# Attention scores of two heads in the two halves of the array's rows, in a two-layer diffusion backbone on one core

## The chip, the cores and the metric

The kernel runs on one core of a Trainium2 chip. Its engines are TensorE (PE, with its weight loads shown apart as PEld), VectorE (DVE), ScalarE (ACT), GpSimd (POOL) and SyncE (SP), which issues most of the transfers from HBM. The metric is the time of one execution on the device, in microseconds.

## The reference

Two layers work on 256 latent tokens and 256 context tokens of 1024 features. A layer is a pair of token mixers (windowed attention with a sink, and a bidirectional gated linear recurrence), gated, projected and normed, and then a mixture of 16 experts, of which each takes 32 tokens of a stream. What matters here is the attention: 8 heads of 64 features, with two groups of keys and values, so that four heads share one set of keys.

```python
HEAD_DIM = 64; ATTN_HEADS = 8; ATTN_KV_HEADS = 2; WINDOW = 128
...
    s_win = jnp.einsum('bntgrd,bnsgd->bngrts', qb, kw) * scale
    s_win = jnp.where(valid[None, :, None, None], s_win, -jnp.inf)
    s_ctx = jnp.einsum('bntgrd,bcgd->bngrtc', qb, kc) * scale
    m = jnp.maximum(jnp.maximum(s_ctx.max(-1), s_win.max(-1)), s_sink)
    ...
    o = (einsum(e_ctx, vc) + einsum(e_win, vw)) / denom
```

A latent token sees its window and the whole context, 512 keys with the mask. A context token (first layer only; the second needs no context output) sees the 256 context keys.

## The kernel before

The function `front(l, ...)` is the mixer of a layer, `moe(l, ...)` its experts. Features lie on the partitions in the mixer: `qT[:, i, :]` holds the queries of heads 2 i and 2 i + 1, the even one on partitions 0 to 63, the odd one on 64 to 127. `kT` holds the keys of a group twice, `kT[:, 2 g]` with the keys on partitions 0 to 63 and zeros below, `kT[:, 2 g + 1]` the other way round. A product of all 128 rows of `qT[:, i]` with one of the two then is the score of one head, the other head meeting zeros. The zeros are written by two memsets in `kv_in`, the keys by four copies in `blk_ka`, two by VectorE and two by ScalarE.

`attention(s, i2, ...)` works on 128 queries of a stream. For each group `g` it takes four heads: the score product into a bank of PSUM (`scb()`, the tag `sc`, two banks), for latent queries the mask (L693), the maximum (L696), the exponential (L701), a scaling (L705), the transposes through another bank (L708) and their copy (L709). After the four heads the products with the values go to a tile `po`, which is also a bank `sc` (L713), and are copied out (L716). The first layer has four such calls, two with 512 keys and two with 256; the second has two with 512. That makes 48 score products.

Most other matmuls in the mixers are `mm3` (L163 to L165): float32 accuracy by three products of split operands. The score products, the transposes and the expert products are plain float32. Several lines divide the array by columns: L713 writes two halves of 64 output partitions, L283 (the modulation, whose steps fill idle times of PE), L527 and L594 write quarters of 32.

The order of the work on each engine's queue is set when the program is built, by a planner that plays the program on a timeline and takes, for an engine that is free, the first ready instruction in the order of the program; `hg_chain` is moved ahead with `tc.high_priority`. Within an engine's queue the order is then fixed. The expert weights are loaded by SyncE in one order (`in_order(loads, ...)`), each as soon as its place is free.

Of the kernel before, what the change touches and what calls it, by code (L numbers as in the profile page):

```python
# [89 lines left out]
def _view(t, offset, pattern):  # L90
    # a strided view of a tile: offset and pattern in elements of one partition
    return bass.AP(tensor=t.tensor, offset=t.offset + offset, ap=[list(t.ap[0])] + pattern)


class HL:
    # a float32 array as the sum of two float32r arrays
# [8 lines left out]
def tile_kernel(ctx, tc, x, c, ctx_in, c_ctx, w_mod, b_mod, w_in, attn_sink, lb_fw, lb_bw, norm_g,  # L105
# [47 lines left out]
    def in_order(chain, ins):  # L153
        # instructions of a chain stay in the order of the program in their engine's queue
        if chain:
            tc.add_manual_dep(ins.ins, chain[0].ins.name,
                              mybir.DependencyInfo(mybir.DependencyClass.NoSync, mybir.DependencyReason.DATA),
                              reason="order")
        chain[:] = [ins]

    def mm3(p, a, b, start, stop, **kw):
        # a^T b in float32 accuracy: the product of the low parts is below its last bit
        mm(p, a.hi, b.hi, start=start, stop=False, **kw)  # L163
        mm(p, a.hi, b.lo, start=False, stop=False, **kw)  # L164
        mm(p, a.lo, b.hi, start=False, stop=stop, **kw)  # L165

    # ---------------------------------------------------------------- constants, small vectors
    # the conditions first: what all else waits on
# [15 lines left out]
    # silu(c), silu(c_ctx) as stationary columns, padded to 32  # L184
# [19 lines left out]
    # lower bounds of the forget gates of the second layer (those of the first are 0): columns (dir, head)  # L204
# [16 lines left out]
    # ---------------------------------------------------------------- modulation, as columns  # L221
    # (section * 2 + half, 128-block, stream); sections 1 and 4 hold 1 + scale
# [11 lines left out]
    def mod_cols(l, pm, a, q0, dq, ns):  # L234
        # chunks q0, q0 + dq: quarters of 256 columns, each on the partitions 32 j + stream
        nc.vector.tensor_copy(a, pm[:, 0:256])
        pt = mdb()
        for m in range(2):
            nc.tensor.transpose(pt[:, 128 * m:128 * m + 128], a[:, 128 * m:128 * m + 128], ident)
        pv = pt[:, 0:256].rearrange("p (m q j r) -> p q j m r", m=2, q=2, j=2)  # L240
        for s in range(ns):
            for q in range(2):
                nc.vector.tensor_tensor(MT[l][:, q0 + dq * q, :, s].rearrange("p (j m) -> p j m", j=2), pv[:, q, :, :, s],
                                        BM[:, l, q0 + dq * q].rearrange("p (j m) -> p j m", j=2), op=ALU.add)

    def mod_first(M0, g):
        # the shifts and scales of a quarter of the features in layer 0
# [19 lines left out]
    def mod_steps(l, q0, ns):  # L267
        # chunks q0, q0 + 1 of the streams: a step for each 128 rows, whose products take PE's idle times
# [24 lines left out]
    def bcast_rows(l, sec, dst, S, after=()):  # L293
        # dst [128, S, 1024]: section 2 (g1) or 5 (g2), the same on every partition
# [10 lines left out]
    # ---------------------------------------------------------------- layer norm  # L305
# [39 lines left out]
    def ln_affine2(dst, src, lnp, mu, r, seq):  # L345
        # from a pair of banks
# [14 lines left out]
    def transposed(xh, s, k, sink_fn, p):  # L361
        # features [128 k, 128 k + 256) of the two token tiles of a stream, modulated by sink_fn
# [49 lines left out]
    # ---------------------------------------------------------------- token mixers  # L412
    def front(l, fillers, X=None, finish=None):
# [16 lines left out]
        # the last of the fillers wait for PE's idle times in the routing  # L430
# [6 lines left out]
        def filler(f):  # L437
            # the transfer of a step runs a step ahead of its products
            if f:
                f[0](WM)  # L440
                behind.append(f[1])
            if len(behind) > 0 or not f and behind:
                behind.pop(0)(WM)
# [29 lines left out]
        def cols_tile(*segs, busy=None):  # L473
            # columns of w_in, in one tile of 256
# [10 lines left out]
        def fm(w, j, n, p=None, ks=range(KT)):  # L485
            # features (128 columns j of the tile w) by n tokens
# [5 lines left out]
        # ---- HGRN: one head  # L492
        # axis of directions: 0 backward, 1 forward
# [18 lines left out]
        def hg_chain(h, q, K, F):  # L512
            # decayed scores, keys by queries: AT (within 128 tokens), A1 (tile to tile), A2 (context to x)
# [9 lines left out]
            def sums(Pr, sel, p, start, stop):  # L523
                # sums over features, to each of the 32 keys of a block that sel takes
# [12 lines left out]
            # level 0: a token with itself, both directions  # L537
# [10 lines left out]
            def update(m):  # L548
                # from blocks of m to blocks of 2 m: decay over the other half
# [18 lines left out]
            # levels 1 and 2: products of single pairs, summed over features  # L568
            for i, m in ((1, 1), (2, 2)):
                p = hsb()  # L570
                for j in range(m):
                    Pr = tp("Pr")[:, :TQ]
                    n = TQ // (2 * m)
                    # queries of a second half with key j of the first half (forward)
                    nc.vector.tensor_tensor(_view(Pr, m, [[2 * m, n], [1, m]]), _view(Q, TQ + m, [[2 * m, n], [1, m]]),
                                            _view(K, 512 + j, [[2 * m, n], [0, m]]), op=ALU.mult)
                    # queries of a first half with key j of the second half (backward)
# [5 lines left out]
            # levels 4, 8, 16: blocks of 32 keys by 32 queries; forward keys in first halves, backward in second  # L583
# [17 lines left out]
            # blocks of 32 and of 64 within a tile  # L601
# [23 lines left out]
            # tile to tile: 0 from the second tile to the first (backward), 1 from the first to the second  # L625
# [8 lines left out]
            # context to x, the sum of both directions  # L634
# [33 lines left out]
        # ---- attention  # L668
# [9 lines left out]
        def attention(s, i2, qT, kT, va):  # L678
# [5 lines left out]
            for g in range(2):  # L684
                eT = C.tile([128, 4, 4, 128], F32, name="eT")
                for i in range(4):
                    hd = 4 * g + i
                    par = i % 2
                    p = scb()
                    mm(p[:, :nk], qT[:, hd // 2, tk], kT[:, 2 * g + par, k0:k0 + nk], start=True, stop=True)  # L690
# [27 lines left out]
        # ---- the schedule of one front  # L718
        C, kT, va, ihv = None, None, None, None

        def chains():
            nonlocal C, kT, va, ihv
            C = pool(sC, f"C{l}")
            kT = C.tile([128, 4, 512], F32, name="kT")
# [8 lines left out]
        def blk_ka(w, j):  # L733
# [4 lines left out]
            for g in range(2):  # L738
                for h in range(2):
                    (nc.scalar.copy if h else nc.vector.tensor_copy)(kT[64 * h:64 * h + 64, 2 * g + h, :],  # L740
# [44 lines left out]
        def kv_in():  # L785
            nc.gpsimd.memset(kT[64:128, 0:4:2, :], 0.0)
            nc.gpsimd.memset(kT[0:64, 1:4:2, :], 0.0)
# [14 lines left out]
        def second(s):  # L802
            # the inputs of the second layer, a stream, in tiles that are free yet; of the context no more is needed
# [57 lines left out]
        else:  # L861
            with ExitStack() as s0:
                xh0 = xh_first(s0)
                M0 = pool(s0, "M0")
                for g in range(5):
# [7 lines left out]
                    # the first head's products as far as the features are there  # L873
                    for i in range(4 if g else 0):
                        fm(ws0[i // 2], i % 2, TQ, ps0[i], range(2 * g - 2, 2 * g))
                # the other constants
# [23 lines left out]
        # ---- branches, gates  # L900
# [59 lines left out]
        # ---- output projection, residual, post norm  # L960
# [11 lines left out]
        # the last token tiles take the first half of w_out first, which is not needed any more then  # L972
# [14 lines left out]
    # ---------------------------------------------------------------- mixture of experts  # L987
    def moe(l, X, M, slots):
# [5 lines left out]
        def eload(src, e):  # L994
            # an expert's matrix in four tiles of 256 rows
# [8 lines left out]
        def eload_cols(src, e):  # L1004
            # an expert's matrix in four tiles of 256 columns
# [15 lines left out]
        # the router's weights for the plain norm of a stream: scaled; the shift's share apart  # L1021
# [12 lines left out]
        def route(s):  # L1034
# [5 lines left out]
            for i in range(2):  # L1040
                t = 2 * s + i
                ln_plain(xh[:, t, :], X[t], i == 0)
                # logits, transposed, in four partial sums; then summed, tokens on partitions
# [27 lines left out]
            # the taken tokens in their order: 1, 2, ..., the others 0  # L1071
# [11 lines left out]
        def onehot(gi, s):  # L1083
            # the slots of the four experts of a group, as one-hot rows of the tokens
# [8 lines left out]
        def weights(gi, s):  # L1093
            # the weighted one-hot rows of a group, slots on partitions
# [7 lines left out]
            if gi == 3 and s == 0:  # L1102
                # the last expert's rows once more, for every share of its products
# [11 lines left out]
        def gather(gi, s, after=()):  # L1115
            # rows of the four experts of a group, feature-major, modulated
# [38 lines left out]
        def end_begin():  # L1155
            # the rows of the first stream with all but the last expert's share
# [9 lines left out]
        def end_products(c, py, hT, w, Yc):  # L1166
            # a quarter of the features of the last expert, the blocks of rows in shares
# [7 lines left out]
        def end_first(c, Yc):  # L1175
            # their share of the first stream
# [7 lines left out]
        def end_second(c, Yc):  # L1184
            # the rows of the second one in their place
# [4 lines left out]
        G = 2 if S == 2 else 4          # column groups of the array  # L1190
        MW = 128 // G                   # slots of an expert (both streams)
        NW = FF // G                    # width of a column group's share
        NB = NW // 128
        for gi in range(4):
            for e4 in range(4):
# [43 lines left out]
                if e == 0:  # L1239
                    late = M["late"]()  # L1240
                    Y, g2 = late["Y"], late["g2"]
                    # g2, its stream as the rows of the products of an expert have it
# [36 lines left out]
        def finish_out():  # L1279
            # the output in halves of the rows, one of them on other engines  # L1280
# [29 lines left out]
    def moe_pools(l, st, S, zones, right=()):  # L1310
        # zones: the pools from the bottom, each a list of names of tiles and of numbers of weight slots
# [4 lines left out]
        for z, names in enumerate((right,) + zones if right else zones):  # L1316
            Z = pool(sZ, f"ZR{l}", side="right") if names is right else pool(st, f"Z{l}{z}")
            for n in names:
                if isinstance(n, int):
                    for i in range(n):  # L1320
                        # the place of WM has 1 KB more than its one slot
                        w = 2304 if z == 2 + (right != ()) else 2048
                        slots.append(lambda Z=Z, i=i, w=w: Z.tile([128, w], F32, name=f"w{i}", tag=f"w{i}")[:, :2048])
                elif n not in shapes:
                    # what is not needed before the end of the first expert: a slot until then
                    once.append(lambda Z=Z, n=n: Z.tile([128, 2048], F32, name="w" + n, tag=n))
                    parts.append((n, lambda Z=Z, n=n: Z.tile([128, 2048], F32, name=n, tag=n)))
                else:
                    M[n] = Z.tile([128] + shapes[n], F32, name=n, tag=n)
                    if n == ("xh" if l else "xs"):  # L1330
                        # the place is free when they are loaded
# [19 lines left out]
    with ExitStack() as st:  # L1351
        M, s, once = moe_pools(0, st, 2, ([4], [2], [1], [3], ["g2 OH", 3], ["xh", 3]), ("Y", "xs", "oT"))
        # the slot in the place of the last modulation's weights comes later than the others
        a, b, c = s[7:10] + s[13:16], s[10:13], s[0:6]
        # in the order of release: the second expert's first products come before the first one's last
# [40 lines left out]
```

## Time and profile before

| | us |
|---|---|
| median of three runs | 1835.53 |
| lowest and highest run | 1832.83, 1835.88 |
| span of the profiled execution (first to last instruction) | 1832.6 |
| PE busy in it | 1579.6 |
| mean granted TensorE clock, as a share of full speed | 0.914 |

The profiled execution's own time outside its span is not recorded; the lowest run is 0.2 us above the span. Stages of that execution: mixer of the first layer to about 460 us, its experts to about 1000, mixer of the second layer to about 1345, its experts to the end.

### The profile page before, as it was taken

What the parts mean: (1) busy time and instruction counts of PE and PEld (TensorE: products, weight loads), DVE (VectorE), ACT (ScalarE), POOL (GpSimd) and SP (SyncE); (2) the same over time, 40 slices, a digit from 0 to 9 for tenths busy, and PEclk for the clock granted to TensorE, in tenths of its full rate; (3) what the DMA queues carried; (4) which work ended last, traced back from release to release, by engine and by line L of the source; (5) the groups of instructions that cost most, each with busy time, mean ns of one, the idle gap of its engine ahead of it and who ended that gap; (6) DMA issues with size and microseconds to landing.
All of it is one profiled execution on the core that took longest, in us unless ns stands there. A gap on an engine that the chain in (4) does not pass through costs nothing. (4 is left out here: it accounts for less than half of the span.)

```text
span 1832.6 us, 27361 instructions
## 1 busy us (share of the span) xinstructions
PE 1579.6 (86%) x11339; PEld 921.2 (50%) x11339; DVE 681.1 (37%) x1425; ACT 449.7 (25%) x850; POOL 304.9 (17%) x300
## 2 busy tenths in 40 slices
PE   6999999999989998997988999998968766766675
PEld 4777776688754433332223788775844322322222
DVE  5546566324651211211213756666651110101102
ACT  2436556323120100001001533576410000000000
POOL 2342121224300000000002633331610000000001
PEclk9999999999989999999999999999978866776777
DMA  9544124524679999999999653325689999999997
GB/s 320 183 117 125 60 81 133 202 91 150 258 300 399 409 409 409 409 409 409 409 409 371 213 174 112 122 81 175 239 341 410 409 409 409 409 408 409 409 409 283
DMA packets 207372, 526.06 MB, mean 287 GB/s; under 512 B 9736, under 2 KB 93904, under 8 KB 207248
## 3 DMA queue, kind: packets, MB, share of 16 engines
q1 hardware_dynamic: 205136, 517.46, 75.3%
q0 software_dynamic: 1392, 4.49, 0.7%
q10 hardware_dynamic: 720, 2.36, 0.4%
q8 instruction: 89, 1.46, 0.3%
q14 instruction: 35, 0.29, 0.0%
HBM read 523.23 MB, written 1.05 MB: 286 GB/s over the span
## 5 line engine op out<-in xcount | busy, mean ns | idle before, releaser
L1204 PE MATMUL acc<-w,xs 128*32 128x256 f32 (+1 forms) x3064 | 419.4, 530 | 102.0 <-DMA w<-in_w_up_dram 56.9
L1204 PEld LDWEIGHTS acc<-w,xs 128*32 128x32 f32 (+1 forms) x3064 | 139.1, 134 | 366.5 <-issue 178.1
L1237 PE MATMUL o<-w,hT 128*32 128x256 f32 (+1 forms) x1432 | 196.5, 534 | 43.0 <-DMA w<-in_w_down_dram 29.2
L163 PE MATMUL acc<-uTh,wh 128*128 128x512 f32 (+1 forms) x592 | 215.0, 365 | 2.4 <-ACT sgs L829 1.5
L164 PE MATMUL acc<-uTl,wh 128*128 128x512 f32 (+1 forms) x592 | 212.0, 358 | 0.5 <-DVE uTl L387 0.5
L165 PE MATMUL acc<-uTh,wl 128*128 128x512 f32 (+1 forms) x592 | 210.7, 356 | 0.0
L1215 ACT ACTIVATE h<-acc 128x512 f32<-128x512 f32 (+1 forms) x32 | 15.7, 490 | 534.2 <-PE acc L1204 521.4
L1237 PEld LDWEIGHTS o<-w,hT 128*32 128x32 f32 (+1 forms) x1432 | 65.8, 136 | 153.2 <-issue 74.0
L468 POOL TENSOR_TENSOR wl<-win,wh 128x1024 fp32r<-128x1024 f32 x44 | 113.7, 2584 | 164.0 <-ACT wh L467 162.4
L1216 DVE TENSOR_TENSOR h<-h,acc 128x512 f32<-128x512 f32 (+1 forms) x32 | 17.7, 552 | 308.7 <-PE acc L1204 308.7
L163 PEld LDWEIGHTS acc<-uTh,wh 128*128 128x128 f32 x592 | 111.8, 190 | 27.0 <-issue 7.1
L165 PEld LDWEIGHTS acc<-uTh,wl 128*128 128x128 f32 x592 | 112.3, 190 | 17.7 <-issue 3.4
L164 PEld LDWEIGHTS acc<-uTl,wh 128*128 128x128 f32 x592 | 112.3, 190 | 17.5 <-issue 3.1
L467 ACT CAST wh<-win 128x1024 fp32r<-128x1024 f32 x84 | 84.0, 1046 | 84.3 <-PE acc L164 61.7
L1096 POOL TENSOR_TENSOR OW<-OH,aff 128x256 f32<-128x256 f32 x8 | 4.9, 615 | 598.5 <-PE sc L1219 583.6
L1260 DVE TENSOR_TENSOR Y<-o,g2 OH 32x512 f32<-32x512 f32 x60 | 41.2, 687 | 141.0 <-PE o L1237 140.3
L468 DVE TENSOR_TENSOR wl<-win,wh 128x1024 fp32r<-128x1024 f32 x40 | 53.5, 1338 | 79.7 <-ACT wh L467 78.9
L1221 ACT COPY hT<-sc 128x512 f32<-128x512 f32 (+1 forms) x32 | 15.3, 479 | 256.1 <-PE sc L1219 256.1
L1260 DVE TENSOR_TENSOR Y g<-o,Y g 32x256 f32<-32x256 f32 x60 | 25.2, 420 | 128.0 <-PE o L1237 127.3
L283 PE MATMUL md<-wmod,scol 128*32 128x256 f32 x640 | 57.6, 414 | 6.6 <-DMA wmod<-in_w_mod_dram 5.2
L553 DVE TENSOR_TENSOR K<-K,F 128x512 f32<-128x512 f32 x56 | 46.6, 832 | 8.7 <-PE hs L619 5.3
L322 POOL TENSOR_TENSOR mv<-mv,nhalf 128x1 f32<-128x1 f32 x26 | 24.4, 943 | 130.6 <-DVE mv L321 125.4
(448 smaller groups left out, 2360.1 us busy)
## 6 DMA issues: line engine op xcount, KB each, us to landing
w<-in_w_gate_dram SPq DMA_DIRECT2D x128, 1024.0 KB, 18.6
w<-in_w_up_dram SPq DMA_DIRECT2D x127, 1024.0 KB, 18.5
w<-in_w_down_dram SPq DMA_DIRECT2D x127, 1024.0 KB, 18.6
wmod<-in_w_mod_dram SPq DMA_DIRECT2D x80, 512.0 KB, 4.6
win<-in_w_in_dram SPq DMA_DIRECT2D x26, 1024.0 KB, 6.3
win<-in_w_in_dram SPq DMA_DIRECT2D x32, 512.0 KB, 5.4
wmod<-in_w_mod_dram SPq DMA_DIRECT2D x32, 256.0 KB, 6.2
wo<-in_w_out_dram SPq DMA_DIRECT2D x8, 1024.0 KB, 5.8
```

What stands on the lines that cost most here:

```text
L163: mm(p, a.hi, b.hi, start=start, stop=False, **kw)
L164: mm(p, a.hi, b.lo, start=False, stop=False, **kw)
L165: mm(p, a.lo, b.hi, start=False, stop=stop, **kw)
L283: mm(pm[32 * j:32 * j + 32, 0:256], scol[:, k, :], w[:, 256 * j:256 * j + 256], start=(k == 0), stop=(k == KT - 1))
L322: pows.append(nc.gpsimd.tensor_tensor(mv[:, 2:3], mv[:, 2:3], nhalf[:, 0:1], op=ALU.pow))
L467: nc.scalar.copy(hi[:, r], w[:, r])
L468: ins = eng.tensor_sub(lo[:, r], w[:, r], hi[:, r])
L553: nc.vector.tensor_tensor(kv, kv, _view(f, 0, [[nf + 1, 2], [2, nf // 2], [0, m]]), op=ALU.mult)
L1204: ins = mm(p[MW * j:MW * j + MW, :NW], xs[:, k, e4, :], wrow(w, k)[:, NW * j:NW * j + NW], start=(k == 0), stop=(k == KT - 1))
L1216: nc.vector.tensor_mul(h, h, pu[:, :NW])
L1237: mm(py[MW * dj:MW * dj + MW, :NW], hT[:, 128 * m + MW * j:128 * m + MW * j + MW], wrow(wd, kt)[:, NW * dj:NW * dj + NW], start=(kt == 0), ...
L1260: nc.vector.tensor_tensor(o, py[r:r + 32, :NW], g2[r:r + 32, NW * dj:NW * dj + NW], op=ALU.mult)
```

## The change

The keys are stored once a group, `kT[0:64, g]` and `kT[64:128, g]` holding the same keys, and there are no zeros and no memsets. The scores of an even head and of the odd one after it are two products of 64 rows, one from partitions 0 to 63 of `qT` and `kT`, the other from 64 to 127, written one after the other in the program ahead of the work on either head, into two banks `sc`. The mask, the softmax, the transposes and the products with the values are as before, head by head. Comments, which the diff also takes out, are left out here.

```diff
@@ attention(s, i2, qT, kT, va)
                 for i in range(4):
                     hd = 4 * g + i
                     par = i % 2
-                    p = scb()
-                    mm(p[:, :nk], qT[:, hd // 2, tk], kT[:, 2 * g + par, k0:k0 + nk], start=True, stop=True)
+                    if par == 0:
+                        sc = [scb(), scb()]
+                        for h in range(2):
+                            r = slice(64 * h, 64 * h + 64)
+                            mm(sc[h][:, :nk], qT[r, hd // 2, tk], kT[r, g, k0:k0 + nk], start=True, stop=True)
+                    p = sc[par]
@@ chains()
-            kT = C.tile([128, 4, 512], F32, name="kT")
+            kT = C.tile([128, 2, 512], F32, name="kT")
@@ blk_ka(w, j)
-                    (nc.scalar.copy if h else nc.vector.tensor_copy)(kT[64 * h:64 * h + 64, 2 * g + h, :],
+                    (nc.scalar.copy if h else nc.vector.tensor_copy)(kT[64 * h:64 * h + 64, g, :],
@@ kv_in()
-            nc.gpsimd.memset(kT[64:128, 0:4:2, :], 0.0)
-            nc.gpsimd.memset(kT[0:64, 1:4:2, :], 0.0)
```

## Rows read from the trace of the kernel before

**Rows 1.** The page: PE's busy share, and PE and DMA in tenths.

```profile
PE 1579.6 (86%) x11339; PEld 921.2 (50%) x11339; DVE 681.1 (37%) x1425; ACT 449.7 (25%) x850; POOL 304.9 (17%) x300
...
PE   6999999999989998997988999998968766766675
...
DMA  9544124524679999999999653325689999999997
```

**Rows 2.** Stretches: us; busy PE, PEld, DVE, ACT, POOL; clock, DMA share, GB/s.

```profile
131.00:300.00 169.00, 169.00 (x1338) 124.67 (x1336) 103.47 (x258) 106.63 (x207) 37.71 (x40) 1.00 0.27 85
300.00:337.00 37.00, 31.03 (x324) 17.50 (x322) 21.79 (x76) 18.88 (x55) 5.23 (x6) 0.91 0.64 199
560.00:990.00 430.00, 388.49 (x1756) 139.09 (x1755) 82.42 (x137) 27.52 (x54) 6.33 (x13) 1.00 1.03 407
1162.00:1276.00 114.00, 106.49 (x877) 75.51 (x875) 74.68 (x202) 77.48 (x153) 26.64 (x30) 0.97 0.38 121
...
1400.00:1832.00 432.00, 290.61 (x2756) 110.22 (x2748) 52.86 (x117) 16.45 (x40) 7.12 (x11) 0.73 1.00 396
```

**Rows 3.** SyncE's waits, 1240 to 1400 us: total us, times, longest.

```profile
SPq L1000 <- PE acc L1204: 31.4, 10, 19.6
```

**Rows 4.** The score line: count, duration ns min/median/max, starts, forms (rows*columns of the array first).

```profile
L690 PE MATMUL sc<-kT,qT x96: 377/592/1061, 131.2 to 1262.5; 128*128 128x512 f32 x64, 128*128 128x256 f32 x32
```

**Rows 5.** Timeline of PE, scores in a row: start us, us, what.

```profile
131.19 1.88 PE L690 MATMUL sc<-kT,qT 128*128 128x512 f32 x4
...
258.08 1.03 PE L690 MATMUL sc<-kT,qT 128*128 128x256 f32 x4
```

**Rows 6.** Timeline of PE: products in the two halves of columns.

```profile
164.21 1.94 PE L713 MATMUL sc<-eT,va 128*64 128x256 f32 x14
```

**Rows 7.** Timeline of PE at changes between full and column-divided products.

```profile
132.06 1.02 PE L690 MATMUL sc<-kT,qT 128*128 128x512 f32 x2
133.01 0.64 PE L283 MATMUL md<-wmod,scol 128*32 128x256 f32 x8
133.58 0.50 PE L163 MATMUL acc<-uTh,wh 128*128 128x512 f32 x1
...
139.31 0.40 PE L163 MATMUL acc<-uTh,wh 128*128 128x512 f32 x1
...
159.39 0.70 PE L690 MATMUL sc<-kT,qT 128*128 128x512 f32 x1
```

**Rows 8.** Timeline of PE at a transpose of 16 rows.

```profile
528.39 0.50 PE L1122 MATMUL o<-OH,xh 128*128 128x128 f32 x3
528.82 0.29 PE L1077 MATMUL hs<-cst,wk 16*128 16x16 f32 x2
...
528.62 0.28 PE L1122 MATMUL o<-OH,xh 128*128 128x128 f32 x1
```

**Rows 9.** Timeline of ACT and PE: exponentials of heads 0, 1, scores of 2, 3.

```profile
135.61 0.69 ACT L701 ACTIVATE e<-sc,v 128x512 f32<-128x512 f32 x1 [0.97 <-DVE v L699]
...
136.47 0.67 ACT L701 ACTIVATE e<-sc,v 128x512 f32<-128x512 f32 x1
...
140.00 1.02 PE L690 MATMUL sc<-kT,qT 128*128 128x512 f32 x2
...
141.31 1.02 PE L690 MATMUL sc<-kT,qT 128*128 128x512 f32 x2
```

**Rows 10.** Timeline of DVE and PE: a group's end, and the last scores.

```profile
166.19 0.42 DVE L716 COPY attnT<-sc 128x256 f32<-128x256 f32 x1 [1.72 <-PE sc L713]
...
167.62 1.88 PE L690 MATMUL sc<-kT,qT 128*128 128x512 f32 x4
...
1261.99 1.13 PE L690 MATMUL sc<-kT,qT 128*128 128x512 f32 x2
```

**Rows 11.** Timeline of GpSimd after the second memset.

```profile
50.27 0.95 POOL L787 MEMSET kT<- 64x1024 f32 x1
61.73 2.42 POOL L468 TENSOR_TENSOR wl<-win,wh 128x1024 fp32r<-128x1024 f32 x1 [10.52 <-ACT wh L467]
```

## Prediction

> **What bounds the kernel now.** I read the page's first two parts first [rows 1]. TensorE (PE) is busy for 86% of the span, but the line of tenths shows two kinds of stretch: nine tenths nearly throughout the first dozen slices, which are the mixers of the first layer, and later long stretches in which the DMA line stands at 9 while PE drops to 6 or 7. The table by stage makes that exact [rows 2]. While the attention of the first layer runs (131 to 300 us) PE is busy 169.00 of 169.00 us, and the DMA engines are used at a quarter. In its tail (300 to 337 us) PE is busy 31.03 of 37, and in the attention of the second layer (1162 to 1276 us) 106.49 of 114. The two expert stages (560 to 990, 1400 to 1832) move 407 and 396 GB/s with the DMA engines full: they are bound by their weights and cannot be shortened by anything in a mixer. They only start earlier or later, because the loads of the first experts take places that the end of a mixer frees.
>
> So a microsecond of PE time in 131 to 300 us counts in full. I count one in the tail by its busy share, 31.03/37 = 0.84, and one in the second layer by 106.49/114 = 0.93. That the shift passes through the expert stages undiminished I take from the queue of the weight loads: around the start of the second layer's experts it waits 31.4 us for PE, 19.6 of it at once [rows 3], so a late PE makes late loads.
>
> **What the score products cost.** The view of the score line shows 96 matmuls, 64 of 512 columns and 32 of 256 [rows 4]: each of the 48 products in float32 is two passes. Their durations there (median 592 ns, shortest 377) hold the latency of the array. What PE gives up is the step from one pass to the next, and the timeline gives it: four passes in a row last 1.88 us, less one duration of 0.59, over three steps: 0.43 us for 512 columns; 1.03 less 0.38, over three: 0.22 us for 256 [rows 5]. All scores together are 64 x 0.43 + 32 x 0.22 = 34.5 us.
>
> **The change, part by part.**
>
> *Two halves side by side.* No row of before shows two products in the two halves of the array's rows. The nearest shows two in the two halves of its columns: 14 passes of 256 columns in 1.94 us [rows 6]. At 0.22 a step in single file they would need 13 x 0.22 + 0.38 = 3.2 us, in pairs 6 x 0.22 + 0.38 = 1.7; so pairs do run together. I take the same for rows: two score products that stand next to each other in PE's queue, one in each half, take two steps in place of four and save 0.86 us (512 columns) or 0.43 (256). From below the bound is nothing saved. An odd head followed by the next even one counts as well as a pair of the code, since they too lie in different halves.
>
> *The boundary.* A product that uses the array in another division than its neighbours pays at each side. Behind the score passes of 132.06 the next pass would start at 132.49 + 0.43 = 132.92; the column-divided one starts at 133.01, 0.09 later, and the full one behind that lasts 0.50 where its like lasts 0.40, which I read as weights that could not be loaded ahead: 0.10 more [rows 7]. A score pass behind a column-divided one lasts 0.70 in place of 0.59 [rows 7]. For rows there is one place: a transpose of 16 rows behind full products [rows 8]. The step before it is (0.50 - 0.28)/2 = 0.11 us, so it was due at 528.72 and started at 528.82: 0.10 late, like the others. I take 0.2 us for each side at which a half-array product meets a full one. The bound from below is nothing, if 64 rows are no division of their own. Where the neighbour is column-divided, the boundary is there already and nothing is added.
>
> The Trainium skill (TensorEngine Tiling (Array Packing), Key Properties) says that changing the tiling mode drains the engine. That is the rule that speaks against this change; it gives no time, and the trace agrees with it by the 0.09 to 0.10 us above; without it the sum would be that of rival D.
>
> *How many stand side by side.* This decides the sign. Before, the products stand on PE in 42 places, the first at 131.19 [rows 5] and the last at 1261.99 [rows 10]; only 6 are doubles (two products in a row), five of 512 columns and one of 256, and 36 are alone. The reason is the two banks `sc`. A product waits until the exponential of an earlier head has read its bank, and those end 0.86 us apart (135.61 and 136.47); the planner then sends each product when its own bank is free: 140.00 and 141.31, with full products between [rows 9]. At the end of a group the output tile `po` takes one bank, so head 0 of the next group goes alone (159.39, [rows 7]) and head 1 follows only when `po` has been copied out at 166.19 (167.62, a double of heads 1 and 2) [rows 10]. The change keeps both banks, their order of use, and every reader. It claims both names at once, but each product still depends on its own bank alone. So I take the order as it is: 6 doubles.
>
> Sides that meet a full product, counted over the same 42 places: 28 in 131 to 300, 6 in the tail, 14 in the second layer. The sum:
> - 131 to 300 us: 28 x 0.2 = 5.6 us added, three doubles of 0.86 and one of 0.43 = 3.0 saved: +2.6, counted in full.
> - tail: 6 x 0.2 = +1.2, times 0.84: +1.0.
> - second layer: 14 x 0.2 = 2.8 added, two doubles of 0.86 = 1.7 saved: +1.1, times 0.93: +1.0.
>
> Together +4.6 us.
>
> *A wait.* Should the planner hold a head's product back to stand beside its partner, or PE reach the second before its bank is free, the second waits at the head of PE's queue, and the full products and transposes behind it wait as well. The price is the 0.86 us between the two exponentials, as much as a double saves; so this moves the sum little, and I take nothing.
>
> *Keys without zeros.* Two memsets of 0.95 us leave GpSimd at the start of each layer's mixer. In the first layer GpSimd then idles until 61.73, waiting for a cast of ScalarE [rows 11]: they are covered, and I count nothing. If something waited behind them the gain would be 1.9 us in each layer; a loss from work left out I exclude. The copies into `kT` stay the same four with the same shapes, so VectorE and ScalarE gain nothing. The tile is 8 KB a partition before and 4 after, and all behind it in its pool moves down; the places that it frees are taken up again long after attention, so I count nothing, with 1 to 2 us of doubt for an order that comes out differently.
>
> **Sum against time.** The profiled execution has a span of 1832.6 us, 2.9 below the median of the three runs (1835.53). With the change: span 1837.2, median 1840.1. From no change a measurement of this kernel can tell about 0.2%, or 3.7 us.
>
> **Rivals.**
> - *B, the pairs find each other* (on the other side). If the planner, with both products next to each other in the program, sends them next to each other, all 24 pairs save: 16 x 0.86 + 8 x 0.43 = 17.2 us, against 24 x 2 sides, of which as before 48 of 84 meet full products: 27 x 0.2 = 5.5. That is -11.7, and by the stages' shares about -11: median 1824.5. From about 11 doubles on the sum turns negative: each double more saves 0.86 and, with one place less, 2 x 48/84 x 0.2 = 0.2 of boundaries. For it: the first two products already do so [rows 5]. Against it: the two banks come free apart [rows 9, 10]. The Trainium skill (TensorE: Matmul & The Clock Gate, Why this matters for your kernels) says that products in distinct row groups run concurrently; that page alone would make this the result. No row of before shows it for rows. Chance 0.16.
> - *C, halves that don't overlap.* Boundaries without savings: 5.6 + 1.0 + 2.6 = +9.2, median 1844.7. For it: no pair of row halves is in the trace; against it, the column halves. Chance 0.12.
> - *D, no boundary for 64 rows.* Savings alone: -3.0 - 1.6 = -4.6, median 1830.9. Against it stands the transpose of 16 rows [rows 8]. Chance 0.12.
> - *E, nothing arrives.* The stalls of tail and second layer take the difference up, or a slightly different order gives it back: within 1 or 2 us of before. For it: PE idles 6 and 7.5 us there [rows 2]; against it, the first stretch has no idle time at all. Chance 0.14.
>
> My forecast A has 0.46, its own range 1837 to 1844.
>
> **How the numbers follow.** A is over the bound of 3.7 us in about 0.29 of its 0.46, C in 0.11: slower 0.40. B gives 0.13 and D 0.08 to faster: 0.21. The rest, 0.39, is no measurable change: E, the lower part of A, the edges of the others. The range runs from 1829.5 (D with a little order for it, a partial B; a full B is left out) to 1846 (C and a microsecond of order).
>
> **What would show each step.** The score matmuls should have 64 rows, still 96. A double should show four passes that start two by two a few ns apart, 0.43 us between the twos; single file in a double means C. A lone product should start 0.1 us late and be followed by a full one of 0.5 us; if both are missing, D. The places on PE should be about 42; near 24 means B. GpSimd should lose four memsets and nothing else. The stretch from 131 us to the end of the first attention should be some 3 us longer, and the loads of the first experts late by as much. I am wrong above all if the planner's order changes: a double more or less is worth 1.1 us.

## The result and the profile after

| | before | after |
|---|---|---|
| median (lowest to highest of 4 runs), us | 1834.53 (1832.83 to 1835.88) | 1844.34 (1843.76 to 1847.76) |
| span of the profiled execution, us | 1832.6 | 1842.8 |
| mean granted TensorE clock | 0.914 | 0.916 |

The change makes the kernel slower, by a ratio of 1.0064 with an interval of 1.0047 to 1.0080. The medians are 9.8 us apart, the spans 10.2. I forecast +4.6: the sign is right and the time lies in the stated range, though above forecast A's own (1837 to 1844), and half of the loss was not in the sum.

The page of after, against [rows 1]: PE's busy time has hardly moved, and GpSimd (POOL) has lost just the four memsets. ScalarE (ACT) has four instructions more, which I did not foresee: loads of function tables, 46 in place of 42, of 1.28 us each.

```profile
PE 1580.0 (86%) x11339; PEld 917.3 (50%) x11339; DVE 673.0 (37%) x1425; ACT 454.4 (25%) x854; POOL 302.7 (16%) x296
...
PE   6999998999989998897988999998968766765665
```

The score line of after, against [rows 4]: 96 matmuls still, now of 64 rows (the first number of a form).

```profile
L694 PE MATMUL sc<-kT,qT x96: 376/589/1219, 130.5 to 1271.5; 64*128 64x512 f32 x64, 64*128 64x256 f32 x32
```

The timeline of PE in after, first at a double, against [rows 5, 7], then at a product that stands alone:

```profile
130.54 1.13 PE L694 MATMUL sc<-kT,qT 64*128 64x512 f32 x4
131.60 0.64 PE L283 MATMUL md<-wmod,scol 128*32 128x256 f32 x8
...
138.68 1.12 PE L694 MATMUL sc<-kT,qT 64*128 64x512 f32 x2
139.74 0.50 PE L163 MATMUL acc<-uTh,wh 128*128 128x512 f32 x1
```

Four passes of a double last 1.13 us where they lasted 1.88: the halves do run together. The two passes of a lone product last 1.12, as long as the four of a double, and a full product of 0.50 follows: the boundary is there. The step between the twos is 0.53 us, not the 0.43 that I expected. Rivals C (no overlap) and D (no boundary) are out. So is B: the 48 products stand in 43 places, and 5 are doubles.

The loss by stages, read off the starts in the two traces: the last score of the first layer starts at 326.9 before and 335.0 after, the first expert product at 534.0 and 542.2, the first score of the second layer at 1162.9 and 1171.2, its last at 1262.5 and 1271.5, and the spans end 10.2 us apart. The first attention loses 8 us, 7 of them in its tail (the first product of its last 128 queries starts at 299.6 before and at 300.3 after). The experts pass them on, the second attention adds 0.7, and what follows it 1.2. The table by stage of after, with the columns of [rows 2], shows where something differs besides the products:

```profile
131.00:300.00 169.00, 169.00 (x1322) 119.77 (x1318) 97.61 (x257) 104.23 (x205) 38.51 (x39) 1.00 0.28 85
300.00:345.00 45.00, 37.94 (x344) 20.89 (x342) 22.75 (x76) 23.27 (x58) 5.75 (x7) 0.85 0.54 169
...
1168.00:1286.00 118.00, 111.04 (x893) 77.68 (x892) 76.12 (x205) 80.32 (x154) 26.51 (x31) 0.93 0.31 99
```

The third number from the end is the granted clock. In the tail of the first attention it is 0.85; in before it is 0.92 over the same 45 us (below), and in the second attention 0.93 against 0.97 [rows 2]. At every moment of these stretches the granted clock is 1.00 or 0.50 (TensorE's 2.4 GHz or 1.2), so a mean of 0.85 over 45 us is 13.5 us at 1.2 GHz, and 0.92 is 7. No term of my sum had this.

### The profile page after: what moved, and what is told of

Its sections match the earlier page's. It is cut to its first block, busy times and chain, and to the rows that moved or that the text cites. A ratio compares the mean times of both kernels' runs of the same rounds, so it can differ in the third digit from the quotient of the medians.

```text
span 1842.8 us, 27357 instructions
## 1 busy us (share of the span) xinstructions
PE 1580.0 (86%) x11339; PEld 917.3 (50%) x11339; DVE 673.0 (37%) x1425; ACT 454.4 (25%) x854; POOL 302.7 (16%) x296
## 5 line engine op out<-in xcount | busy, mean ns | idle before, releaser
L1207 PE MATMUL acc<-w,xs 128*32 128x256 f32 (+1 forms) x3064 | 410.1, 519 | 102.8 <-DMA w<-in_w_up_dram 60.5
L1240 PE MATMUL o<-w,hT 128*32 128x256 f32 (+1 forms) x1432 | 195.2, 527 | 46.1 <-DMA w<-in_w_down_dram 31.7
```

The costliest lines, as they stand in the source:

```text
L1207: ins = mm(p[MW * j:MW * j + MW, :NW], xs[:, k, e4, :], wrow(w, k)[:, NW * j:NW * j + NW], start=(k == 0), stop=(k == KT - 1))
L1240: mm(py[MW * dj:MW * dj + MW, :NW], hT[:, 128 * m + MW * j:128 * m + MW * j + MW], wrow(wd, kt)[:, NW * dj:NW * dj + NW], start=(kt == 0), ...
```

## The experiments

Below, a difference in us is the ratio with its interval times 1833; every run stands beside runs of the kernel before on the same chip. Single executions of one kernel lie up to some 5 us from its median, so a span or a clock of one profile is read with that in mind, and the differences rest on the repeated runs. The first theories were 'halves' (the boundary is dearer than 0.2 us a side) and 'order' (PE's queue came out in another order, which costs by itself).

### Halves alone, order alone

e1_half_singly: each product where it stood in the program before; as in the change, the keys are stored once and there are no memsets.

```diff
-                    mm(p[:, :nk], qT[:, hd // 2, tk], kT[:, 2 * g + par, k0:k0 + nk], start=True, stop=True)
+                    r = slice(64 * par, 64 * par + 64)
+                    mm(p[:, :nk], qT[r, hd // 2, tk], kT[r, g, k0:k0 + nk], start=True, stop=True)
```

> Products of 64 rows, keys stored once, but each head's product is written in the program where it stood before, so PE's queue is that of the kernel before, instruction for instruction: 42 places, 6 doubles, 48 sides that meet a full product. Theory 'halves' (all of the +9.8 us of the change comes from the half-array products, whose boundary is dearer than 0.2 us a side): +8 us or more, span about 1841. Theory 'order' (half-array products cost about the forecast's +4.6, which the score rows of the changed kernel bear out with +4.3 and +2.0 us less one double and four sides; the rest comes from another order of PE's queue): +4 to +5.5 us, span about 1837.

e2_full_pairs: the pairs of the change, with full products, zeros and memsets.

```diff
-                            r = slice(64 * h, 64 * h + 64)
-                            mm(sc[h][:, :nk], qT[r, hd // 2, tk], kT[r, g, k0:k0 + nk], start=True, stop=True)
+                            mm(sc[h][:, :nk], qT[:, hd // 2, tk], kT[:, 2 * g + h, k0:k0 + nk], start=True, stop=True)
```

> Products of all 128 rows with the zero halves and the four memsets, as before, but the two products of a pair stand next to each other in the program, as in the changed kernel. In the first layer PE's queue is that of the changed kernel; no half-array product is left. Theory 'halves': 0 us, span about 1832.6, since the order costs nothing. Theory 'order': +3.5 to +5 us, span about 1837, with the first attention ending some 4 us later than before, and the longer stretch at half clock in its tail.

Measured: e1 +9.7 us (7.0 to 12.3), e2 +4.0 (2.0 to 6.0). Each theory hits one and misses the other. e2 is less than the change's order alone, though: PE's queue is that of the change only up to 311 us, in the tail it is its own, and in the attention of the second layer it is that of before. Since e1 has the queue of the kernel before, its 42 places can be set beside those of before, one by one. I take the time from the start of the instruction ahead of a place to the start of the second behind it, in e1 less before:

```
lone, both sides full products       10 places   +0.34 to +0.40 us
lone, one side full                  17 places   +0.15 to +0.20
lone, both sides column-divided       3 places    0.00
double of 512, no / one / two full    1, 2, 2    -0.86, -0.66, -0.46
double of 256, two full                1         -0.04
(6 more places stand at half clock in one of the two, +0.5 together)
sums of all 42: latent queries of layer 0 +0.90; context, first 128 +1.52, second 128 +0.87;
      layer 1, first 128 queries +0.44, second 128 +0.57; together +4.30
```

The timelines of one place of each kind show it. In e1, a lone product between full ones, and one between column-divided ones:

```profile
138.45 0.40 PE L165 MATMUL acc<-uTh,wl 128*128 128x512 f32 x1
138.78 1.12 PE L691 MATMUL sc<-kT,qT 64*128 64x512 f32 x2
139.83 0.50 PE L163 MATMUL acc<-uTh,wh 128*128 128x512 f32 x1
140.17 0.40 PE L164 MATMUL acc<-uTl,wh 128*128 128x512 f32 x1
...
228.74 1.12 PE L691 MATMUL sc<-kT,qT 64*128 64x512 f32 x2
229.80 0.64 PE L283 MATMUL md<-wmod,scol 128*32 128x256 f32 x8
```

The same in before (its score product of 140.00 stands in [rows 9]):

```profile
139.77 0.39 PE L165 MATMUL acc<-uTh,wl 128*128 128x512 f32 x1
...
141.08 0.39 PE L164 MATMUL acc<-uTl,wh 128*128 128x512 f32 x1
...
229.03 1.12 PE L690 MATMUL sc<-kT,qT 128*128 128x512 f32 x2
230.09 0.64 PE L283 MATMUL md<-wmod,scol 128*32 128x256 f32 x8
```

From 139.77 to 141.08 are 1.31 us, from 138.45 to 140.17 1.72: two sides, 0.41. Between column-divided neighbours the step is 1.06 in both. So the price of a side (0.2 us), the gain of a double (0.86) and the free place are what I forecast, and their sum is +4.3 against my +4.6 (+4.9 before the two discounts). Theory 'halves' falls in the form in which I gave it; yet e1 loses 9.7 us, with no other order. Something besides the places takes 5 us.

The windows of before, e1 and e2 over the tail of the first attention and over the later part of the second (granted clock third from the end):

```profile
300.00:345.00 45.00, 38.99 (x367) 22.68 (x366) 27.93 (x86) 23.68 (x64) 6.65 (x8) 0.92 0.68 219
1225.00:1285.00 60.00, 53.90 (x447) 36.57 (x448) 35.63 (x111) 36.89 (x79) 9.15 (x11) 0.94 0.46 157
```

```profile
300.00:345.00 45.00, 40.61 (x373) 22.38 (x372) 24.12 (x78) 23.88 (x63) 7.03 (x8) 0.81 0.56 174
1225.00:1285.00 60.00, 53.53 (x408) 31.67 (x406) 32.33 (x105) 36.75 (x78) 8.12 (x12) 0.86 0.30 97
```

```profile
300.00:345.00 45.00, 39.15 (x349) 22.08 (x341) 23.25 (x75) 24.11 (x59) 6.70 (x7) 0.85 0.60 191
1225.00:1285.00 60.00, 51.88 (x433) 34.72 (x433) 36.71 (x115) 37.83 (x80) 9.38 (x12) 0.94 0.43 146
```

PE is busy about as long in each of the three, but e1 runs at a lower clock in both stretches, and e2, whose order differs, in the first. That gave the next theory, 'clock': half-array products in stretches where PE's queue is thin (in both, PE of the kernel before is idle for 6 us) keep TensorE at 1.2 GHz longer. Its rivals were 'shift' (any delay of a microsecond or two upsets those stretches) and 'layout'.

### Pairs made to stand together

e3_gated_pairs and e4_gated_full make rival B real: the even head's product gets one more dependence, on what frees the odd head's bank.

```diff
+                            if h == 0 and freed:
+                                tc.add_manual_dep(ins.ins, freed[0].ins.name, ...)
...
-                    nc.scalar.activation(e[:, :nk], p[:, :nk], AF.Exp, ...)
+                    freed[:] = [nc.scalar.activation(e[:, :nk], p[:, :nk], AF.Exp, ...)]
...
-                nc.vector.tensor_copy(attnT[:, 2 * g:2 * g + 2, tk], ...)
+                freed[:] = [nc.vector.tensor_copy(attnT[:, 2 * g:2 * g + 2, tk], ...)]
```

> The changed kernel, with one dependence more: the even head's product also waits for what frees the odd head's bank (the exponential of the odd head before, or the copy of the output tile), so the two become ready together. 23 of 24 pairs then stand side by side, with 26 sides that meet full products. Rival B of the forecast made real. By the prices of the forecast: 15 x 0.86 + 8 x 0.43 = 16.3 us saved, 5.2 added: 11 us faster than before, some 1823, if the held-back products cost nothing. If the later start of the even head stretches the attention where PE has idle time (its tail in the first layer, the second layer), the gain is smaller by what PE idles more there, and the time may be at or above that of before.

> The pairs of e3_gated_pairs with the same dependence, but products of all 128 rows with zero halves and memsets: in the first layer the same queue of PE. The difference between the two is what the halves save when nearly all stand side by side: by the forecast's prices 10.3 - 3.6 = 6.7 us in the first layer and 6.0 - 1.6 = 4.4 in the second, so this kernel should be some 10 us slower than e3_gated_pairs. Against the kernel before it shows the price of the held-back order alone: near 0 if a saturated PE always has other work, +3 us or more if the order of the tail decides.

Measured: e3 +26.6 us (23.3 to 29.7), e4 +31.7 (29.3 to 34.1). The medians are 1859.67 and 1863.56, so the halves gain 3.9 us, not 10. A pair of e3 on the timeline of PE, two steps in place of four, as it should be, and PE by stages:

```profile
207.36 1.13 PE L696 MATMUL sc<-kT,qT 64*128 64x512 f32 x4
208.42 0.50 PE L163 MATMUL acc<-uTh,wh 128*128 128x512 f32 x1
```

```profile
131.00:300.00 169.00, 163.01 (x1386) 118.91 (x1386) 100.39 (x249) 98.67 (x187) 42.85 (x41) 0.99 0.30 96
300.00:360.00 60.00, 45.49 (x328) 24.17 (x327) 21.71 (x90) 25.39 (x76) 3.52 (x5) 0.80 0.48 151
```

The copies of the output tiles in the first layer (first and last start) in before, then in e3:

```profile
L716 DVE COPY attnT<-sc x8: 410/423/425, 166.2 to 336.1; 128x256 f32<-128x256 f32 x8
```

```profile
L727 DVE COPY attnT<-sc x8: 405/424/425, 164.4 to 356.5; 128x256 f32<-128x256 f32 x8
```

The first group is as early as ever, the last 20 us late. A held-back product is the first link of a chain (score, exponential, transposes, values, copy) on which the next group waits. PE has other work for some of that time, but then idles 6 us in the first stretch, which had no idle time, and 14.5 of 60 in the tail. With two banks for scores, these runs could feed the pairs or the chain, not both.

### Which part of the halves costs

All of these have PE's queue of the kernel before, with zeros and memsets. Only the products named are of 64 rows:

```diff
+                    r = slice(64 * par, 64 * par + 64) if (l, s) == (0, 0) else slice(0, 128)
+                    mm(p[:, :nk], qT[r, hd // 2, tk], kT[r, 2 * g + par, k0:k0 + nk], start=True, stop=True)
```

The condition is `(l, s) == (0, 0)` in e5, `(0, 1)` in e6, `l == 1` in e7, the six doubles in e8, and none (all are of 64 rows) in e9.

> PE's queue, the layout of the keys and the memsets of the kernel before; products of 64 rows only for the 16 products of latent queries in the first layer (131 to 245 us, where PE has no idle time and the granted clock is full). In e1_half_singly these 16 cost 1.0 us more than before, place by place. Theory 'clock' (half-array products let TensorE stay at half clock longer where its queue holds little work; that makes the rest of e1's +9.7): +1 us, since the tail is as before. Theory 'shift' (any microsecond of delay changes the tail and the second layer by a few us): +4 us or more.

> As e5_latent_l0, but 64 rows only for the 16 products of context queries in the first layer (249 to 327 us, with the tail). Place by place they cost 2.4 us more in e1_half_singly. Theory 'clock': +4 to +5 us, with some 17 us at half clock between 300 and 345 us where the kernel before has 6.8. Theory 'shift': +2.4, give or take 2, with 6.8 us at half clock.

> As e5_latent_l0, but 64 rows only for the 16 products of the second layer. Place by place they cost 0.9 us more in e1_half_singly. Theory 'clock': +3.5 to +4.5 us, with 17 us at half clock between 1160 and 1290 us in place of 6.8. Theory 'shift': +1. The three parts together should make the +9.7 us of e1_half_singly; if their sum is far smaller, the memsets and the layout of the keys, which these three keep as before, have a price too.

> PE's queue of the kernel before; products of 64 rows only for the 12 that stand as six doubles, full ones for the 36 that stand alone. Place by place those six save 0.66, 0.47, 0.46, 0.04, 0.66 and 0.85 us in e1_half_singly: 3.1 us. Both theories: 1 to 3 us faster than before, if the half-array products in the doubles don't change the clock; theory 'clock' allows part of it to be given back in the second layer, where one double stands beside a stretch at half clock.

> The products of 64 rows of e1_half_singly, in PE's queue of the kernel before, but the keys are stored as before, four copies with zero halves and the four memsets. Theory 'clock': as e1_half_singly, +8 to +11 us, with 14 us or more at half clock in the tail of the first attention and about 17 in the second layer. Theory 'layout' (the other place of the pool's tiles or GpSimd's missing work makes a part of e1's price): +4 to +5 us, the sum of the places.

e10 is the changed kernel with `kT[r, 2 * g + h]`, zeros and memsets.

> The changed kernel with the keys stored as before, zero halves and memsets included; PE's queue is that of the changed kernel. Theory 'clock' with 'order': as the changed kernel, +9 to +12 us; GpSimd has its four memsets again and nothing gets later by them. Theory 'layout': +5 us or less.

e11 to e15 split e6 and e7 by queries: `l == 1 and i2 == 0`, `l == 1 and i2 == 1`, `(l, s, i2) == (0, 1, 0)`, `(0, 1, 1)`, and all products but those of e12 and e14.

> As e7_layer1, but 64 rows only for the 8 products of the first 128 queries of the second layer (1162 to 1213 us), ahead of the stretches at half clock. Place by place they cost 0.5 us more. Theory 'clock': +0.5 us, and 3.4 to 7 us at half clock between 1160 and 1290 us, as before. Theory 'shift': as e7_layer1, about +2.

> As e7_layer1, but 64 rows only for the 8 products of the second 128 queries of the second layer (1226 to 1263 us), among the stretches at half clock. Place by place they cost 0.4 us more at full clock. Theory 'clock': +2 to +3.5 us, with about 17 us at half clock between 1160 and 1290 us. Theory 'shift': +0.4, or anything, with 6.8 us at half clock.

> PE's queue, keys and memsets of the kernel before; products of 64 rows only for the 8 of the first 128 context queries of the first layer (249 to 286 us, where PE has no idle time). Place by place they cost 1.5 us more. Theory 'clock': +1.5 us. If the extra of e6_context_l0 (+5.5 against places of 2.4) lies here, +4.

> As e13_context_first, but only the 8 products of the second 128 context queries (300 to 327 us, the tail of the first attention). Place by place they cost 0.9 us more. Theory 'clock': +2.5 to +4 us and 10 us or more at half clock between 300 and 345 us, where the kernel before and the others with full products there have 0 to 6.8. If the tail's clock doesn't depend on them: +0.9.

> Products of 64 rows for 32 of the 48, all but those of the second 128 context queries of the first layer (its tail) and of the second 128 queries of the second layer. Place by place they cost 3.0 us more. Theory 'clock': +3 us, with the times at half clock of the kernel before. If the extra of e1_half_singly does not come from the two stretches left out: +6 us or more.

Measured; "places" is the sum of the places from above, the last two columns the granted clock of the one profiled execution:

| run | us more than before | places | clock 300 to 345 | clock 1225 to 1285 |
|---|---|---|---|---|
| before | | | 0.92 | 0.94 |
| e5, latent, layer 0 | +0.7 (-0.9 to 2.4) | 0.9 | 0.92 | 0.97 |
| e6, context, layer 0 | +5.5 (3.1 to 8.1) | 2.4 | 0.92 | 0.94 |
| e13, its first 128 queries | +0.5 (-1.3 to 2.4) | 1.5 | 0.92 | 0.97 |
| e14, its second 128, the tail | +3.8 (2.2 to 5.3) | 0.9 | 0.77 | 0.91 |
| e7, layer 1 | +2.7 (1.1 to 4.4) | 1.0 | 0.92 | 0.86 |
| e11, its first 128 queries | -0.5 (-2.6 to 1.3) | 0.4 | 0.96 | 0.97 |
| e12, its second 128 | +3.1 (1.3 to 4.9) | 0.6 | 1.00 | 0.86 |
| e15, all but e14's and e12's | +1.3 (-0.4 to 2.7) | 2.9 | 0.96 | 0.97 |
| e8, the doubles alone | -2.0 (-3.8 to -0.2) | -3.1 | 0.89 | 0.94 |
| e9, all, with zeros | +11.4 (8.8 to 13.9) | 4.3 | 0.89 | 0.86 |
| e10, the change, with zeros | +10.6 (8.2 to 12.8) | | 0.92 | 0.86 |

Three readings follow.

*Layout, memsets and, with the halves in place, the new order cost and gain nothing that these runs can tell.* e9 and e1, and e10 and the changed kernel, agree within their intervals. So do e9 and e10, which differ in the order alone (PE's queue of e10 is that of the changed kernel): their medians, beside the same runs of before, are 1843.80 and 1844.00 us.

*Outside two stretches, places cost no more than their sum.* e5, e13, e11 and e15 are at or a little below theirs: 32 products of 64 rows, two thirds of all, cost +1.3 us together.

*In two thin stretches 16 products cost 7 us, with places of 1.4.* e14 and e12 each lie above their places, by 2.9 and 2.5 us, and 'shift' falls: the places of e15 delay PE more than theirs and upset nothing. In the second layer the rows agree with 'clock'. The six profiles in which all eight products of the second 128 queries are of 64 rows (e1, e7, e9, e10, e12 and after) have 0.86 there, 17 us at 1.2 GHz; the nine with full ones, or in e8 six full and one double of halves (before, e2, e5, e6, e8, e11, e13, e14, e15), have 0.91 to 0.97. From the first of these products to the last copy of an output tile the six take 53.8 to 54.4 us, the nine 48.2 to 50.8. e3 and e4 stand apart: their attention comes 20 to 30 us later, and over the 60 us from the first of these products they have 0.89 with halves and 0.86 with full products, so in that order the halves don't decide it. The split by queries, e11 and then e12:

```profile
1225.00:1285.00 60.00, 53.95 (x470) 37.55 (x469) 35.13 (x110) 35.68 (x78) 9.53 (x12) 0.97 0.49 167
```

```profile
1225.00:1285.00 60.00, 53.95 (x421) 33.36 (x420) 33.09 (x106) 33.41 (x72) 7.78 (x10) 0.86 0.44 150
```

PE is busy for the same 53.95 us in both, but it gets through 421 matmuls in place of 470: busy is not fast. Against before, e12 has 10 us more at 1.2 GHz, worth at most 5 us of PE's work, and takes 54.4 us for the stretch in place of 49.7. So in the profiles the clock carries the cost here; why the halves keep it low is not shown.

In the tail of the first layer the clock scatters more. In before's queue, full products there have 0.89 to 1.00, 64-row products 0.77 to 0.92. e14 and e15:

```profile
300.00:345.00 45.00, 39.57 (x333) 21.90 (x328) 22.32 (x76) 21.47 (x58) 5.46 (x7) 0.77 0.57 177
```

```profile
300.00:345.00 45.00, 38.57 (x371) 22.11 (x368) 28.31 (x85) 24.31 (x65) 7.02 (x8) 0.96 0.66 214
```

Here e14 had its expected 20 us at 1.2 GHz, but e6, with the same products in the tail, had 7 in its profile, as many as before, where its expectation said 17, and e9 had 10 for its 14 or more. The mean clock of each execution is on record too. Over the runs of e14 it is 0.9145, over those of before beside them 0.9204: 22 us more at 1.2 GHz, give or take some 10; over those of e15 it is 0.9204. The runs of e6 show no such thing (0.9195 against 0.9198), nor do e7 (0.9201 against 0.9198) and e12 (0.9186 against 0.9195) their 10 us; these means hold over 200 us at 1.2 GHz of the last expert stage, and 10 us are about what they can tell.

The repeated runs place the cost in the tail; that the clock carries it there is borne out by e14, not by e6, and stays open. In the new order the tail grows without it: in e10 its scores start from 300.0 to 334.0 us, in before from 299.6 to 326.9, with as many us at 1.2 GHz:

```profile
300.00:345.00 45.00, 36.40 (x346) 20.60 (x346) 23.55 (x76) 23.94 (x60) 6.68 (x7) 0.92 0.55 175
```

e8 is the only version whose interval lies below the kernel before: halves where two products already stand together, full products elsewhere. It gains 2.0 us of its 3.1, at the edge of what can be measured.

## Why the prediction was right and wrong

*Right: what a product costs.* The overlap of the halves, 0.86 us a double, 0.2 us a side and none at a column-divided neighbour came out place by place, with +4.3 against +4.6. The Trainium skill (TensorEngine Tiling (Array Packing), Key Properties) says that a change of mode drains the engine; 0.10 us of late start and 0.10 of a load that nothing covers is what these rows give it.

*Right: most of the small print.* Memsets and layout count nothing (e9, e10), the experts pass the delay on, and PE full between 131 and 300 us pays no more than its places (e5, e13).

*Wrong, but not what the time turned on: "I take the order as it is".* Written as a pair, the products come out in 43 places with 5 doubles, 38 sides on full products in the first layer in place of 34. By the same prices this is 0.86 + 4 x 0.2 = 1.7 us more. e2 has no half-array product and loses 4.0 us, where I allowed 1 to 2 of doubt; its profile shows the loss in the tail, at a clock of 0.85. Yet with the order just as I assumed it, the halves lose +9.7 (e1) and +11.4 (e9), no less than with the new one, +10.6 (e10), so this step does not explain the miss. By single profiles, the new order loses in the tail (34.0 us from the first score to the last in e10, 28.8 in e9) and wins some of it back in the second layer (60.2 us from the first score of its first 128 queries to that of its second, 62.7 in e9), where e2 has the order of before. Its four more table loads may have a part in the tail; that was not tried.

*Wrong: "I count one in the tail by its busy share".* This is the step that failed. I discounted the two stretches with idle time, by 0.84 and 0.93, as if a microsecond there were partly absorbed. The discounts themselves are 0.3 us of the sum; what failed is the premise that idle time can only make a product cheaper. The dear products are just there: +3.8 us for a tail that I put at +1.0 (e14), +3.1 for eight products of the second layer, whose sixteen I put at +1.0 together (e12). In the order of before this closes the account: 4.3 for the places and 2.9 + 2.5 beyond them make 9.7, against 9.7 in e1 and 11.4 in e9. My rows of before already showed 0.91 and 0.97 for these stretches [rows 2], and I used them for nothing.

*A number that fits for the wrong reason.* Rival C gave 1844.7, and 1844.3 was measured; its mechanism, halves that don't overlap, is refuted by each double.

*Rival B* was the other sign, and e3 shows why its dependence does not bring it about: waiting for the partner's bank costs the chain far more than a double saves.

What stays open: the split by stretches was made in the order of before. In the new order the places come to 6.0 and the total is the same, but which part falls to its longer tail and which to the clock was not taken apart. Nor was it tried whether the products of the two stretches would cost only their places at an undisturbed clock.

## What to carry to other kernels

Two half-array products are worth writing as a pair only where they will stand next to each other in the engine's queue; alone, each pays 0.2 us at every side on a full product, which two sides turn into half of what a double saves. Look at the queue of the built program, not at the source, and mix the forms: halves in the doubles, full products elsewhere (e8, whose gain of 2.0 us is at the edge of what can be measured). And don't discount a stretch because the engine has idle time in it: look at its granted clock first; half-array products cost about five times their places in two such stretches here (7 us for 1.4).

## What the runs showed of the hardware

- Two float32 products in the two halves of the rows last 1.13 us in place of 1.88 for 512 columns. Beside a boundary their two steps take 1.06 us, 0.53 each, where full passes in a row take 0.43.
- A 64-row product between column-divided neighbours costs what a full one does there, 1.06 us from its start to the next.
- In one stretch of 60 us, the granted clock was 0.86 in all six profiles with eight products of 64 rows and 0.91 to 0.97 in the nine with at most two; e11 (0.97) and e12 (0.86) have the same busy time.
